# Planning an instruction order with longer elementwise durations and fewer reserved PSUM banks

## The chip, the cores and the metric

The kernel runs on one core of one Trainium2 chip. The metric is the device time of one launch in microseconds (us), as the median of three timed runs. A profile is one more execution, recorded by the hardware; its engines are called PE (TensorE, matrix products), PEld (its weight loads), DVE (VectorE), ACT (ScalarE), POOL (GpSimd) and SP (the queue that issues the DMAs).

## The reference

Two networks run one after the other on 512 tokens of width 1024, two layers each. In the first, a layer mixes latent attention (8 heads) with a gated depthwise convolution of 31 taps, and is followed by a gated feed-forward of width 2816. The second has a state-space mixer in its first layer, a gated recurrence (HGRN2) in its second, and after each a squared-ReLU feed-forward of width 4096 and a gate by an embedding. Cut to what matters:

```python
for l in range(DEPTH):
    p = _rmsnorm(x, g_mix[l]) @ w_in[l]
    c_q, c_kv = _rmsnorm(p[..., :o1], g_q[l]), _rmsnorm(p[..., o1:o2], g_kv[l])
    y_attn = _mla_attention(q_nope, q_rope, k_nope, k_rope, v)      # from c_q @ w_uq, c_kv @ w_ukv
    u = _dwconv(a * jax.nn.sigmoid(gt), w_dw_conv[l], b_dw_conv[l])  # 31 taps
    u = jax.nn.silu(_layernorm(u, g_conv_ln[l], b_conv_ln[l]))
    x = x + jnp.concatenate([y_attn, u], axis=-1) @ w_o[l]
    z = _dwconv(_rmsnorm(x, g_ffn[l]) @ w_up[l], w_dw_ffn[l], b_dw_ffn[l])
    x = x + (jax.nn.silu(zg) * zv) @ w_down[l]
x = _rmsnorm(x, g_final)
for i in range(DEPTH):
    mix = ssd_mixer(x, ...) if i % 2 == 0 else hgrn2_mixer(x, ...)
    h = layer_norm(ALPHA * x + mix, ...)
    h = layer_norm(ALPHA * h + relu(h @ w1)**2 @ w2, ...)
    x = h + jax.nn.sigmoid(h @ ple_w_gate[i]) * (p[i] @ ple_w_proj[i])
```

## The kernel before

All activations are held transposed: 128 channels on the partitions, 512 tokens along a row, so the stream X is eight tiles of 128x512. A weight block comes by one DMA into one of three buffers of class `r` (the function `weights`, line 687) and is then split into a high part, a cast to the rounded format fp32r (`copy`, line 684: on ScalarE or on VectorE), and a low part, the difference (`either.tensor_sub`: on GpSimd or on VectorE). A dense product is, per 128 rows of weight, three matmuls (high by high, high by low, low by high) that add up in one PSUM bank: 24 for a full sum over 1024 channels. When its sum is complete, VectorE or ScalarE reads the bank.

Nothing is issued while the network is written down. The class `Recorder` only notes operations with the tiles that they read and write, and `schedule` (line 462) then plans all 19,079 of them: it holds a time at which each engine is free, takes again and again the ready operation that could start earliest (ties and near ties by a priority made of recording order and length of what follows), adds its planned cost, and hands out the buffers. `issue` (line 587) emits the instructions in that order, so every elementwise instruction, matmul and DMA in the profile stands on line 597. On the chip each engine works off its own queue in the planned order and waits where the order makes it wait; the plan's times are not used any further.

Three things in the planner matter here. First, `cost` (line 342) gives the planned duration of an operation on ScalarE, VectorE or GpSimd; `cost_tensor` gives that of matmuls and is another function. Second, an operation recorded with `either`, `other` or `any` may run on one of two engines; the second of them is taken only if the operation ends there no later than it would on the first, by what is already queued on both. In this way casts go between ScalarE and VectorE, and two-source additions, subtractions and products between GpSimd and VectorE. Third, `KEEP` (line 616) says how many of a class's free buffers a younger operation must leave for tiles that were recorded earlier and have none yet; there are eight PSUM banks, and the number kept is four.

In the attention part, a head pair runs through Q and K products, score blocks of 128x512 (three matmuls into a bank), a minimum over a row on VectorE, an exponential on ScalarE, transposes on TensorE, copies out of PSUM, and the products with V. Beside it `conv_tile` (line 976) works off the convolution: 17 taps accumulate in a PSUM bank on VectorE (SCALAR_TENSOR_TENSOR psum<-u,V,psum), 14 are multiplied on ScalarE (ACTIVATE s<-u,V) and added by GpSimd or VectorE. The output projection follows, first for the attention's half, then for the convolution's half after a normalisation. In the recurrence (`hgrn`, line 1316), every head forms decay products over six levels before its small matmuls. Normalisations over 1024 channels and the last projection before them are done in two halves of 256 tokens.

Of the kernel before, what the change touches and what calls it, by code (L numbers as in the profile page):

```python
# [232 lines left out]
class Tl:  # L233


    def __init__(self, cls, shape, dt):
        self.cls, self.shape, self.dt = cls, tuple(shape), dt
        self.acc, self.left, self.slot, self.real, self.pe = [], 0, None, None, None
        self.touch = {}
# [80 lines left out]
class Recorder:  # L320
# [9 lines left out]
    def __init__(self):  # L330
        self.ops, self.bias, self.label, self.switch = [], 0, "", 150
        self.greed, self.order_w, self.second, self.eager, self.drag = 0.015, 1.0, 0, 0, 0.5

    def tile(self, cls, shape, dt=F32):
        return Tl(cls, shape, dt).ap()
# [4 lines left out]
        return _Eng(self, eng)  # L340

    def cost(self, eng, meth, args, kw):
        out = kw.get("out", args[0] if args else None)
        n = out.n if isinstance(out, Ap) else 1
        every = [a for a in list(args) + list(kw.values()) if isinstance(a, Ap)]
        ps = any(a.tl.cls == "psum" for a in every)
        ptr = sum(isinstance(a, Ap) and a.n == 1 for a in args[1:]) + sum(isinstance(kw.get(k), Ap) for k in ("scale", "bias"))
        if eng == "scalar":
            return (51 if ps else 93) + 0.833 * n + 93 * (ptr + ("accum_out" in kw))
        if eng == "vector":  # L350
            if meth == "reciprocal":
                return 70 + 6.3 * n
            if meth in ("tensor_scalar", "tensor_copy") and not ps:
                return 69 + 0.52 * n + 60 * ptr
            if meth == "tensor_reduce":
                n = kw["in_"].n
            return 69 + 1.041 * n + 60 * ptr
        if eng == "gpsimd":
            if kw.get("op") == ALU.pow:
                return 298 + 165 * n  # L360
            if meth == "memset":
                return 36 + n
            if meth == "tensor_copy":
                return 120 + 3.4 * n
            return 147 + 2.105 * n
        return 60
# [32 lines left out]
    def any(self, *forms):  # L399

        eng, meth, args, kw = forms[0]
        self.add(eng, meth, args, kw)
        self.ops[-1].alts = [(e, self.cost(e, m, a, k), [(m, a, k)]) for e, m, a, k in forms]
        self.ops[-1].shared = {e: self.shares(e, m, a, k) for e, m, a, k in forms}
# [208 lines left out]


SLOTS = {"psum": 8, "r": 3, "s": 86, "u": 4, "t": 12, "n": 24, "V": 1, "C": 1}
KEEP = {"psum": 4, "s": 18, "u": 2, "t": 6, "n": 16}
SIDE_TAPS = 14
EARLY = 3
FILL = {"mlp0": [(0, 0)], "mlp1": [(1, 0)]}
# [994 lines left out]
def build(tc, xT, pos, wts, vecs, consts, pT, outT, dbg=None, stop=None):  # L1614
    R = Recorder()
    record(R, xT, pos, wts, vecs, consts, pT, outT, dbg, stop)
    R.schedule(SLOTS, KEEP)
    with tc.manual_schedule(), tc.tile_pool(name="sbuf", bufs=1) as sb, \
# [37 lines left out]
```

## Time and profile before

| | us |
|---|---|
| median of three timed runs (2746.51 to 2747.91) | 2747.29 |
| profiled execution, its own time | 2746.72 |
| its span, first to last instruction | 2744.9 |
| TensorE busy in the span | 2680.1 |
| VectorE busy | 1878.6 |
| ScalarE busy | 1176.4 |
| GpSimd busy | 775.2 |

The mean granted clock of TensorE is 0.995 of full speed; a view by stretch ends each row with that clock, the DMA share and GB/s. A group of instructions is read as: line, engine, operation, what is written and read by buffer class (`s` tiles of up to 2 KB a partition, `r` raw weights, `u` padded rows, `n` and `t` small ones, `V` per-channel vectors, `C` constants, `psum`), size and count. Matmuls overlap in the records, so a busy TensorE is not always one at its full rate. The profile's slices show a nearly full TensorE everywhere; the places where it is not full are two stretches near the start and near 700 us, and parts of 1200 to 1450 and 1950 to 2350 us.

### The profile page before, as it was taken

Reading aid. Unit: us, or ns where it says so; the run is one execution under the profiler, and the core shown is the slowest. Engines: PE = TensorE matmul, PEld = TensorE weight load, DVE = VectorE, ACT = ScalarE, POOL = GpSimd, SP = SyncE. Lnnn points to the kernel's source line nnn. Section 1 sums busy time; section 2 is a strip of 40 time slices with the busy share of each in tenths; the row PEclk is TensorE's granted clock in tenths of the full one; section 3 lists DMA queues with packets and bytes.
Section 4 is the critical chain, followed back from the end, with each engine's and each line's share of the span. In section 5 each row is a group of like instructions: output and inputs, shape, how many; then the busy total and the mean of one; then the engine's idle time right before and its main releaser. Section 6 shows DMA issues by size and latency. Waiting matters only on the chain.

```text
span 2744.9 us, 38876 instructions
## 1 busy us (share of the span) xinstructions
PE 2680.1 (98%) x15054; PEld 2213.4 (81%) x15054; DVE 1878.6 (68%) x3319; ACT 1176.4 (43%) x2151; POOL 775.2 (28%) x645
## 2 busy tenths in 40 slices
PE   9899999999899999999989999999999999999998
PEld 7668888888678888888768898888888889888888
DVE  8997676666977766675885675445677887554546
ACT  4874323345764332343653432222356664322223
POOL 1771010134840111242331421222412123112232
PEclk9999999999999999999999999999999999999999
DMA  5031233231131223331112413223131113232320
GB/s 171 18 108 69 76 103 107 99 111 30 56 108 54 93 92 108 99 103 47 40 62 73 163 55 103 91 101 109 62 108 48 60 66 114 88 108 83 115 93 32
DMA packets 69448, 234.98 MB, mean 86 GB/s; under 512 B 7824, under 2 KB 11152, under 8 KB 69264
## 3 DMA queue, kind: packets, MB, share of 16 engines
q1 hardware_dynamic: 69264, 232.51, 25.3%
q8 instruction: 118, 1.93, 0.3%
q14 instruction: 66, 0.54, 0.1%
HBM read 230.38 MB, written 2.10 MB: 85 GB/s over the span
## 4 chain that ended last, share of the span: by engine, by line
PE 80%; DVE 15%; issue 3%; ACT 2%; POOL 0%; DMA 0%; POOLq 0%; DVEq 0%; ACTq 0%; SPq 0%
PE psum L597 80%; DVE s L597 10%; DVE psum L597 3%; ACT s L597 1%; DVE n L597 1%; ACT L597 0%; DMA r<-wts 0%; POOL n L597 0%; POOL s L597 0%; DVE u L597 0%; DVE t L597 0%; POOL u L597 0%; ACT t L597 0%; POOLq L597 0%; DVEq L597 0%
## 5 line engine op out<-in xcount | busy, mean ns | idle before, releaser
L597 PE MATMUL psum<-s,s 128*128 128x512 f32 (+3 forms) x12944 | 2604.2, 365 | 35.8 <-DVE s L597 16.0
L597 PEld LDWEIGHTS psum<-s,s 128*128 128x128 f32 (+1 forms) x12944 | 2117.8, 185 | 472.8 <-issue 27.3
L597 POOL TENSOR_TENSOR s<-r,s 128x512 fp32r<-128x512 f32 (+1 forms) x342 | 469.4, 1389 | 1062.2 <-ACT s L597 798.7
L597 ACT CAST s<-r 128x512 fp32r<-128x512 f32 (+1 forms) x721 | 407.9, 611 | 402.3 <-DMA r<-wts 390.4
L597 DVE TENSOR_TENSOR s<-s,s 128x256 f32<-128x256 f32 (+5 forms) x625 | 405.8, 672 | 76.7 <-ACT s L597 66.1
L597 DVE TENSOR_TENSOR s<-s,psum 128x512 f32<-128x512 f32 (+2 forms) x400 | 224.0, 591 | 297.6 <-PE psum L597 297.2
L597 POOL TENSOR_TENSOR s<-s,s 128x512 f32<-128x512 f32 (+4 forms) x215 | 257.1, 1206 | 514.2 <-DVE s L597 348.3
L597 DVE TENSOR_TENSOR s<-r,s 128x512 fp32r<-128x512 f32 (+1 forms) x527 | 378.2, 746 | 5.9 <-ACT s L597 3.4
L597 ACT ACTIVATE s<-s 128x512 f32<-128x512 f32 (+1 forms) x338 | 186.5, 579 | 211.8 <-DVE s L597 210.6
L597 ACT ACTIVATE s<-u,V 128x512 f32<-128x512 f32 x200 | 142.5, 763 | 264.8 <-DVE u L597 264.6
L597 ACT ACTIVATE s<-psum 128x512 f32<-128x512 f32 (+2 forms) x174 | 91.7, 528 | 373.6 <-PE psum L597 370.3
L597 DVE SCALAR_TENSOR_TENSOR s<-u,V,s 128x512 f32<-128x512 f32 x176 | 143.1, 814 | 50.0 <-ACT s L597 46.8
L597 DVE SCALAR_TENSOR_TENSOR s<-psum,s 128x512 f32<-128x512 f32 (+1 forms) x88 | 55.3, 639 | 113.4 <-ACT s L597 109.4
L597 DVE TENSOR_TENSOR u<-psum,s 128x512 f32<-128x512 f32 x88 | 60.6, 689 | 83.0 <-PE psum L597 82.8
L597 POOL TENSOR_TENSOR n<-n,n 128x4 f32<-128x4 f32 (+1 forms) x32 | 35.0, 1095 | 282.1 <-DVE n L597 281.6
L597 ACT COPY s<-psum 128x512 f32<-128x512 f32 (+4 forms) x137 | 69.6, 531 | 86.2 <-PE psum L597 85.2
L597 ACT CAST s<-s 128x512 fp32r<-128x512 f32 (+2 forms) x125 | 72.7, 592 | 75.4 <-DVE s L597 74.7
L597 DVE CAST s<-r 128x512 fp32r<-128x512 f32 (+1 forms) x148 | 62.7, 434 | 54.5 <-DMA r<-wts 54.3
L597 ACT ACT_TABLE_LOAD x68 | 87.2, 1283 | 21.2 <-DVE s L597 19.3
L597 PE MATMUL psum<-C,s 128*128 128x128 f32 (+1 forms) x532 | 80.3, 271 | 12.7 <-ACT s L597 6.0
L597 DVE SCALAR_TENSOR_TENSOR psum<-u,V,psum 128x512 f32<-128x512 f32 x128 | 91.3, 743 | 0.3
L597 PEld LDWEIGHTS psum<-C,s 128*128 128x128 f32 x532 | 63.6, 146 | 30.7 <-ACT s L597 12.8
(87 smaller groups left out, 875.3 us busy)
## 6 DMA issues: line engine op xcount, KB each, us to landing
r<-wts SPq DMA_DIRECT2D x415, 512.0 KB, 3.6
r<-wts SPq DMA_DIRECT2D x12, 256.0 KB, 2.8
r<-wts SPq DMA_DIRECT2D x8, 384.0 KB, 3.1
s<-xT SPq DMA_DIRECT2D x8, 256.0 KB, 6.1
s<-pT SPq DMA_DIRECT2D x8, 256.0 KB, 4.0
outT<-s SPq DMA_DIRECT2D x16, 128.0 KB, 1.8
r<-wts SPq DMA_DIRECT2D x9, 128.0 KB, 2.0
V<-vecs SPq DMA_DIRECT2D x1, 480.5 KB, 6.6
```

Of the source, the lines that this page charges most:

```text
L597: getattr(eng, meth)(*[res(a) for a in args], **{k: res(v) for k, v in kw.items()})
```

## The change

A new attribute `margin` of 1.1 multiplies the planned duration of everything on ScalarE, VectorE and GpSimd. The old formulas move unchanged into `duration`; the cost of matmuls and of DMAs stays as it is. `KEEP` for PSUM goes from four to two. Nothing else is edited, so the operations recorded are the same, and their order and, where there is a choice, their engine are planned anew.

```diff
--- before.py
+++ after.py
@@ -330,6 +330,7 @@
     def __init__(self):
         self.ops, self.bias, self.label, self.switch = [], 0, "", 150
         self.greed, self.order_w, self.second, self.eager, self.drag = 0.015, 1.0, 0, 0, 0.5
+        self.margin = 1.1
 
     def tile(self, cls, shape, dt=F32):
         return Tl(cls, shape, dt).ap()
@@ -340,6 +341,11 @@
         return _Eng(self, eng)
 
     def cost(self, eng, meth, args, kw):
+
+        return self.duration(eng, meth, args, kw) * (1.0 if eng == "sync" else self.margin)
+
+    @staticmethod
+    def duration(eng, meth, args, kw):
         out = kw.get("out", args[0] if args else None)
         n = out.n if isinstance(out, Ap) else 1
         every = [a for a in list(args) + list(kw.values()) if isinstance(a, Ap)]
@@ -613,7 +619,7 @@
 
 
 SLOTS = {"psum": 8, "r": 3, "s": 86, "u": 4, "t": 12, "n": 24, "V": 1, "C": 1}
-KEEP = {"psum": 4, "s": 18, "u": 2, "t": 6, "n": 16}
+KEEP = {"psum": 2, "s": 18, "u": 2, "t": 6, "n": 16}
 SIDE_TAPS = 14
 EARLY = 3
 FILL = {"mlp0": [(0, 0)], "mlp1": [(1, 0)]}
```

What the new plan does is seen in the order in which instructions stand on an engine. A name is a buffer class and a number that tells tiles apart; the numbers differ between the two kernels.

VectorE in the first layer, up to the addition that completes the sum of squares of the key-value latent (`s_885<-s_885,s_922` in the last row). `psum_620` and `psum_691` are the convolution's accumulators of channel tiles 0 and 1; `s_908<-psum_749,V_65,s_890` is the low part of a latent. Before:

```order
L597 SCALAR_TENSOR_TENSOR psum_620<-u_71,V_65,psum_620 128x512
L597 SCALAR_TENSOR_TENSOR psum_691<-u_67,V_65,psum_691 128x512
L597 SCALAR_TENSOR_TENSOR psum_620<-u_71,V_65,psum_620 128x512
L597 TENSOR_TENSOR s_585<-s_585,s_737 128x512
L597 SCALAR_TENSOR_TENSOR psum_620<-u_71,V_65,psum_620 128x512
L597 TENSOR_SCALAR n_905<-psum_887 128x4
L597 SCALAR_TENSOR_TENSOR s_908<-psum_749,V_65,s_890 128x512
L597 TENSOR_TENSOR n_905<-n_905,n_525 128x4
L597 SCALAR_TENSOR_TENSOR psum_620<-u_71,V_65,psum_620 128x512
L597 SCALAR_TENSOR_TENSOR psum_691<-u_67,V_65,psum_691 128x512
L597 TENSOR_SCALAR n_905<-n_905 128x4
L597 TENSOR_TENSOR s_885<-s_885,s_922 128x512
```

The same place with the change; the addition is `s_863<-s_863,s_891` in the last row, `psum_603` the accumulator of channel tile 0:

```order
L603 TENSOR_SCALAR s_391<-s_391,V_65 128x512
L603 TENSOR_SCALAR s_449<-s_449,V_65 128x512
L603 SCALAR_TENSOR_TENSOR s_857<-s_758,V_65,s_391 128x512
L603 SCALAR_TENSOR_TENSOR s_865<-s_789,V_65,s_449 128x512
L603 TENSOR_TENSOR s_873<-r_555,s_802 128x512
L603 TENSOR_SCALAR n_878<-psum_860 128x4
L603 SCALAR_TENSOR_TENSOR s_880<-psum_731,V_65,s_869 128x512
L603 SCALAR_TENSOR_TENSOR psum_603<-u_71,V_65,psum_603 128x512
L603 TENSOR_TENSOR n_878<-n_878,n_681 128x4
L603 TENSOR_TENSOR s_863<-s_863,s_891 128x512
```

Fewer convolution taps stand ahead of that addition; it was instruction 153 of VectorE's queue and is 139. The rotary tables (`s_391`, `s_449`) are finished later than before.

TensorE at the end of the attention of layer 1. `psum_7080` takes the last products of probabilities and V, `psum_7139` the convolution's mean, `psum_7169` and `psum_7181` are the first sums of the output projection. Before:

```order
L597 MATMUL psum_7130<-C_156,s_7111 128x128 x4
L597 MATMUL psum_7139<-s_6663,t_78 128x512
L597 MATMUL psum_7080<-s_7120,s_6115 64x256
L597 MATMUL psum_7080<-s_7132,s_6115 64x256
L597 MATMUL psum_7080<-s_7120,s_6210 64x256
L597 MATMUL psum_7080<-s_7132,s_6210 64x256
L597 MATMUL psum_7080<-s_7123,s_6226 64x256
L597 MATMUL psum_7080<-s_7136,s_6226 64x256
L597 MATMUL psum_7080<-s_7123,s_6233 64x256
L597 MATMUL psum_7080<-s_7136,s_6233 64x256
L597 MATMUL psum_7169<-s_6497,s_6398 128x512
L597 MATMUL psum_7169<-s_6527,s_6398 128x512
```

The same place with the change: the products go to `psum_7052`, the convolution's mean to `psum_7102`, the output projection's sums are `psum_6920` and `psum_7112`:

```order
L603 MATMUL psum_7093<-C_152,s_7076 128x128 x4
L603 MATMUL psum_7102<-s_7065,t_78 128x512
L603 MATMUL psum_7112<-s_6490,s_6475 128x512
L603 MATMUL psum_6920<-s_6737,s_6475 128x512
L603 MATMUL psum_7112<-s_6498,s_6475 128x512
L603 MATMUL psum_7052<-s_7087,s_6164 64x256
L603 MATMUL psum_7052<-s_7106,s_6164 64x256
L603 MATMUL psum_7052<-s_7087,s_6170 64x256
L603 MATMUL psum_7052<-s_7106,s_6170 64x256
L603 MATMUL psum_7052<-s_7095,s_6185 64x256
L603 MATMUL psum_7052<-s_7110,s_6185 64x256
```

Matmuls of the output projection now stand ahead of the last products of attention; the very first of `psum_6920` stands 77 instructions further up.

GpSimd in the recurrence, at its last heads. Rows with `r` are low parts of weights, `n` a power of four columns, a shape of three numbers is an operation on half of a tile's columns. Before:

```order
L597 TENSOR_TENSOR s_20300<-s_20300,s_20180 128x64x4
L597 TENSOR_TENSOR n_20391<-n_20386,n_74 128x4
L597 TENSOR_TENSOR s_20425<-r_20176,s_20419 128x512
L597 TENSOR_TENSOR s_20653<-s_20653,s_20514 128x512
L597 COPY s_20704<-s_20657 128x256
L597 TENSOR_TENSOR s_20704<-s_20708,s_20786 128x256
L597 TENSOR_TENSOR n_20932<-n_20928,n_74 128x4
L597 TENSOR_TENSOR s_20939<-r_20359,s_20757 128x512
L597 TENSOR_TENSOR s_20962<-r_20538,s_20804 128x512
L597 TENSOR_TENSOR n_21122<-n_21110,n_74 128x4
```

The same heads with the change:

```order
L603 TENSOR_TENSOR s_20285<-s_20285,s_20195 128x16x16
L603 TENSOR_TENSOR n_20396<-n_20387,n_74 128x4
L603 TENSOR_TENSOR s_20355<-s_20355,s_20195 128x8x32
L603 TENSOR_TENSOR s_20433<-s_20417,n_20293 128x4x64
L603 TENSOR_TENSOR s_20671<-r_20281,s_20655 128x512
L603 COPY s_20693<-s_20543 128x256
L603 TENSOR_TENSOR s_20735<-s_20735,s_20543 128x32x8
L603 TENSOR_TENSOR n_20928<-n_20925,n_74 128x4
L603 TENSOR_TENSOR s_20824<-s_20824,s_20543 128x8x32
L603 TENSOR_TENSOR s_20954<-s_20931,n_20766 128x4x64
L603 TENSOR_TENSOR s_20970<-s_20941,n_20766 128x4x64
L603 TENSOR_TENSOR n_21118<-n_21103,n_74 128x4
```

More of the heads' half-tile products stand on GpSimd, which were on VectorE.

## Rows read from the trace of the kernel before

**Rows 1.** The page: TensorE's busy time; the chain that ended last, by engine.

```profile
PE 2680.1 (98%) x15054; PEld 2213.4 (81%) x15054; DVE 1878.6 (68%) x3319; ACT 1176.4 (43%) x2151; POOL 775.2 (28%) x645
...
PE 80%; DVE 15%; issue 3%; ACT 2%; POOL 0%; DMA 0%; POOLq 0%; DVEq 0%; ACTq 0%; SPq 0%
```

**Rows 2.** Stretches: from, to, length, busy us (instructions) of PE, PEld, DVE, ACT, POOL.

```profile
45.00:200.00 155.00, 141.20 (x719) 104.79 (x719) 152.28 (x238) 119.64 (x233) 104.93 (x85) 0.98 0.16 54
200.00:640.00 440.00, 439.95 (x1917) 357.72 (x1916) 294.87 (x439) 155.35 (x256) 74.76 (x62) 1.00 0.28 95
640.00:750.00 110.00, 101.50 (x503) 78.41 (x501) 102.79 (x160) 82.88 (x155) 82.01 (x70) 1.00 0.10 31
750.00:800.00 50.00, 47.81 (x278) 36.08 (x279) 39.12 (x62) 35.13 (x74) 27.42 (x20) 1.00 0.30 98
...
1200.00:1440.00 240.00, 228.87 (x1317) 183.58 (x1316) 184.75 (x389) 125.55 (x203) 84.97 (x70) 0.99 0.15 49
2030.00:2280.00 250.00, 241.62 (x2986) 207.70 (x2985) 191.87 (x463) 169.68 (x326) 55.96 (x42) 0.99 0.21 69
```

**Rows 3.** What TensorE waited for, whole span: us in total, times, longest us.

```profile
PE psum L597 <- DVE s L597: 24.9, 30, 3.3
PE psum L597 <- ACT s L597: 15.6, 23, 1.7
...
PE psum L597 <- POOL s L597: 4.3, 7, 1.1
```

**Rows 4.** The same, 45 to 200 us.

```profile
PE psum L597 <- ACT s L597: 5.7, 7, 1.1
PE psum L597 <- DVE s L597: 4.9, 3, 3.3
```

**Rows 5.** The same, 640 to 800 us.

```profile
PE psum L597 <- ACT s L597: 4.0, 6, 1.7
...
PE psum L597 <- POOL s L597: 1.2, 2, 0.7
```

**Rows 6.** The same, 1200 to 1440 us.

```profile
PE psum L597 <- DVE s L597: 6.9, 10, 1.1
```

**Rows 7.** The same, 2030 to 2280 us.

```profile
PE psum L597 <- issue: 6.5, 3, 2.5
```

**Rows 8.** Timeline near 96 us: start, us, engine, instruction [idle before <- releaser].

```profile
95.80 0.67 DVE L597 TENSOR_TENSOR s<-s,s 128x512 f32<-128x512 f32 x1
...
96.52 1.05 PE L597 MATMUL psum<-C,s 128*128 128x1 f32 x8 [3.35 <-DVE s L597]
```

**Rows 9.** Timeline near 697 us.

```profile
696.99 1.09 PE L597 MATMUL psum<-C,n 128*128 128x128 f32 x8 [3.32 <-DVE n L597]
```

**Rows 10.** Groups of VectorE by shape, whole span: busy us, mean ns | idle before.

```profile
L597 DVE TENSOR_TENSOR s<-r,s 128x512 fp32r<-128x512 f32 x518 | 374.8, 752 | 5.9 <-ACT s L597 3.4 <-PE psum L597 0.5
...
L597 DVE TENSOR_TENSOR s<-s,s 128x256 f32<-128x256 f32 x196 | 87.0, 471 | 28.8 <-ACT s L597 24.6 <-POOL s L597 2.8
L597 DVE CAST s<-s 128x512 fp32r<-128x512 f32 x89 | 64.1, 720 | 4.1 <-DVE s L597 0.5
L597 DVE CAST s<-r 128x512 fp32r<-128x512 f32 x146 | 62.1, 436 | 53.5 <-DMA r<-wts 53.3
```

**Rows 11.** Groups of GpSimd and ScalarE by shape, whole span.

```profile
L597 POOL TENSOR_TENSOR s<-s,s 128x512 f32<-128x512 f32 x111 | 155.2, 1409 | 156.8 <-DVE s L597 89.2 <-ACT s L597 52.8 <-PE psum L597 10.7
L597 POOL TENSOR_TENSOR s<-s,s 128x256 f32<-128x256 f32 x50 | 41.1, 832 | 123.9 <-DVE s L597 67.6 <-ACT s L597 56.3
...
L597 ACT ACT_TABLE_LOAD x68 | 87.2, 1283 | 21.2 <-DVE s L597 19.3 <-PEq L1648 0.7
```

**Rows 12.** Timeline near 108 us: a VectorE subtraction beside GpSimd.

```profile
106.62 2.58 POOL L597 TENSOR_TENSOR s<-s,s 128x512 fp32r<-128x512 f32 x2 [1.57 <-DVE s L597]
106.73 1.41 DVE L597 SCALAR_TENSOR_TENSOR psum<-u,V,psum 128x512 f32<-128x512 f32 x2
...
108.05 1.72 DVE L597 TENSOR_TENSOR s<-r,s 128x512 fp32r<-128x512 f32 x1
```

## The prediction

> **What bounds the kernel now.** I read the page first: TensorE is busy 98% of the span, and the chain that ended last lies on it for 80% and on VectorE for most of the rest [rows 1]. So elementwise durations can only matter where TensorE is not fed, and the second view, busy time by stretch, says where that is [rows 2]. In 200 to 640 us, mostly the first feed-forward, TensorE has no gap worth naming and VectorE is busy 67%; the other three feed-forward parts look alike. No order of elementwise work can win time there. The first attention with its convolution (45 to 200 us) is different: VectorE is busy 152.3 of 155 us, TensorE 141.2. The second one begins alike (640 to 750: 102.8 of 110), with a loose end (750 to 800: 39.1 of 50). The state-space block (1200 to 1440) has VectorE at 77% and TensorE idle for 11.1 us; the gated recurrence (2030 to 2280) has 8.4 us of idle TensorE.
>
> The third view is what TensorE waited for. Of its waits VectorE's tiles ended 24.9 us, ScalarE's 15.6 and GpSimd's 4.3 [rows 3]. In the first attention 4.9 us end on VectorE and 5.7 on ScalarE [rows 4]; but VectorE itself is idle only 2.7 us there, so ScalarE's lateness is mostly VectorE's, one step back, and in this stretch time is what VectorE has queued. A row shows it: the four-column sums of the key-value latent start at 96.52 us after 3.35 us of idle TensorE, released by an addition that VectorE began at 95.80 [rows 8], behind convolution taps that nobody waits for yet. At 696.99 us the same happens in the second layer, 3.32 us [rows 9].
>
> **The change part by part.** No operation is added or removed, only placed. Counted along the queues, VectorE has 3200 instructions instead of 3319, ScalarE 2044 instead of 1987 (table loads apart), GpSimd 703 instead of 641, TensorE and the DMA queue as many as before. So planning with longer elementwise durations makes VectorE's backlog look longer and sends casts to ScalarE and two-source operations to GpSimd.
>
> *First attention.* Ahead of the last subtraction of attention 0, VectorE has 297 instructions instead of 310. 37 are gone: 11 casts and copies, 25 two-source operations, one small copy. 24 came: 6 casts (one of half width) and 18 two-source (one of half width). A two-source operation takes 0.75 us, a cast 0.44 (from a weight buffer) to 0.72 (from a tile), mean 0.58 [rows 10]. So 5.5 x 0.58 = 3.2, and 7.5 x 0.75 = 5.6: 8.8 us less. TensorE's work up to that point is the same to two matmuls. Since VectorE has 2.7 idle us of 155, nothing hides this; I take 7, as the chain score, minimum, exponential, transposes keeps some of it (ScalarE ends seven of TensorE's waits there [rows 4]). Bounds 0 and 8.8.
>
> *Second attention.* Between the last residual of the first feed-forward and the last subtraction of attention 1 it is 226 instead of 236: 34 gone (15 casts, 19 two-source), 24 came (7 and 17, one half): 8 x 0.58 + 2.5 x 0.75 = 6.5 us. Only the first two thirds are bound by VectorE [rows 2], so I take 4.5. Bounds 0 and 6.5.
>
> *State-space block.* 358 instead of 372 between the second feed-forward and the last result of the block: ten two-source and four casts fewer, some 7.5 us of VectorE. It is not full there; TensorE waits 6.9 us for it [rows 6]. I take 2, bounds 0 and 6.9.
>
> *Gated recurrence.* VectorE loses 32 instructions, GpSimd gains 12, most of them half-width products of the decay levels. Of the 8.4 us that TensorE idles there 6.5 are "issue", which has no elementwise releaser [rows 7]. Value 0; what this side can lose is a rival below.
>
> *Two banks kept instead of four.* TensorE may open younger sums while older ones are still to come. The places are the ends of attention, where output-projection matmuls now stand ahead of the last score block's products. A 512-column matmul costs 0.23 us (1917 instructions in 440 us [rows 2]), and the ones moved are a handful, all paid anyway: their worth is that they fill gaps already counted above. Zero by itself, bounds -2 and +2.
>
> *Table loads.* 72 instead of 68, 1.28 us each [rows 11]: 5.1 us of ScalarE, two of them in the state-space block and two in the recurrence, where ScalarE has 114 of 240 and 80 of 250 us free [rows 2]. Nothing; 5.1 if that cover were gone.
>
> *Normalisations and start.* VectorE's queue has the same operations, a few swapped. Outside the first attention and the state-space block TensorE waits 24.9 - 4.9 - 6.9 = 13.1 us for VectorE's tiles [rows 3, 4, 6], most of it here. Value 0, and I allow 4 either way, a third of that.
>
> The sum: 7 + 4.5 + 2 = 13.5 us. The profiled execution took 2746.72 us, 1.8 of it outside its span of 2744.9, and lies 0.6 below the median of the three timed runs. 2746.7 - 13.5 = 2733.2, with the median's offset 2733.8; I say 2733.5.
>
> **The rivals.** *A: VectorE's share comes off whole.* 8.8 + 6.5 + 6.9 = 22.2 us, 2725. For it: VectorE's 98% in the first attention. Against: the second is loose after 750 us.
>
> *B: no change.* VectorE gets done sooner and then waits for scores, as the chain through TensorE, VectorE's minimum, ScalarE's exponential and the transposes sets the pace. Then all terms are zero: 2747. For it: ScalarE ends 5.7 us of TensorE's waits in attention and 4.0 in the second [rows 4, 5]. Against: with VectorE at 98% there is no sign of a pace that is not its own.
>
> *C: GpSimd becomes the late one, slower.* A two-source operation takes 1.41 us there against 0.75 [rows 10, 11], so each moved one comes 0.66 later to its reader, and while it runs VectorE can be held: a two-source operation that started beside one took 1.72 instead of 0.75 [rows 12]. Moved to GpSimd are 21 in the first attention and 18 in the second (18 and 16 others come back). If the moved ones are on the chain: 21 x 0.66 - 8.8 = +5.1, 18 x 0.66 - 6.5 = +5.4, and 13 half-width products of the recurrence at 0.83 instead of 0.47 [rows 10, 11]: +4.7. Together +15.2: 2762. It decides once GpSimd has no free time before a reader needs it: it is busy 104.9 of 155 and 82.0 of 110 us [rows 2], so a third is free. Against it also: TensorE waited for GpSimd's tiles 1.2 us in the second attention [rows 5] and 4.3 in the whole span, and GpSimd's queue up to its last operation of attention 0 is two instructions shorter than before.
>
> The Trainium skill (SBUF, "Who interferes with whom") says that a VectorE instruction with two SBUF inputs and a GpSimd instruction that reads SBUF exclude each other, the first one holding the pair of ports for its whole length; the row of 1.72 us agrees. By that rule, if the pair of ports were what fills the first attention, a net three operations moved to GpSimd would lengthen it by 3 x 0.66 = 2.0 us instead of winning 7, and the sum would be 2742; it is a mild form of C and has its chance there. Against it stands a row: two taps, which read one tile and a PSUM bank, took 1.41 us beside GpSimd [rows 12], 0.7 each, so much of VectorE's work in attention does not meet GpSimd's.
>
> **How the numbers follow.** Forecast 0.55, A 0.12, B 0.15, C 0.18. The forecast's own range is 2726 to 2741, gains of 6 to 21 of the 22.2 that the bounds allow. The range of 8 in 10 reaches over B to the weaker half of C, in which only one attention stretch and the recurrence pay: 2720 to 2754. This kernel's runs agree to some 0.05%, and 0.2% (5.5 us) is what I take as told from no change: faster is under 2741.8. A and nearly all of the forecast give 0.66; B with the forecast's weak end 0.16; C 0.18.
>
> **What will show it.** If right: TensorE's wait of 3.35 us at 96.5 and of 3.32 at 697 are gone or halved; the transposes that stood at 696.99 us stand some 8 us earlier, 7 from the first attention and the rest from their own; VectorE is still over 93% busy in the first attention; TensorE has no gaps in the feed-forward parts, as before. Wrong: VectorE under 90% there with no shorter stretch (B); TensorE's waits for GpSimd's tiles grown from 4.3 us to over 12, or the recurrence longer than 255 us (C). Those transposes at 697 us or later would break the main term.

## The result, and the profile after

The changed kernel takes 2721.65 us (median of four runs, 2720.93 to 2726.2), the kernel before, run beside it, 2746.9 (2743.84 to 2747.91). The ratio is 0.9913, 95% interval 0.9896 to 0.9931: faster by 0.9%, or 25 us. The forecast was 2733.5 in a range of 2720 to 2754, so the time lies in the lower end of the range: below the forecast's own range (2726 to 2741), and some 3 us below rival A (2725).

The profiled execution of the changed kernel is the slowest of its four, 2726.2 us with a span of 2724.4. The traces therefore show 20.5 of the 25 us. The page after, where [rows 1] showed the page before:

```profile
PE 2672.7 (98%) x15054; PEld 2214.5 (81%) x15054; DVE 1835.5 (67%) x3200; ACT 1216.5 (45%) x2212; POOL 851.9 (31%) x707
...
PE 91%; DVE 6%; issue 1%; ACT 1%; DMA 1%; POOL 0%; SPq 0%; POOLq 0%; DVEq 0%; ACTq 0%
```

VectorE's part of the chain that ended last fell from 15% to 6%. By stretch, answering to [rows 2] (from, to, length, busy us of PE, PEld, DVE, ACT, POOL with their counts, granted clock, DMA share, GB/s); the bounds are moved to about where the same work lies now:

```profile
45.00:188.00 143.00, 135.29 (x712) 102.19 (x712) 137.87 (x223) 115.70 (x224) 101.37 (x82) 1.00 0.12 41
188.00:628.00 440.00, 439.86 (x1920) 358.24 (x1919) 299.78 (x438) 164.43 (x273) 89.02 (x70) 1.00 0.30 101
628.00:728.00 100.00, 97.63 (x484) 76.10 (x483) 88.67 (x143) 78.04 (x147) 68.44 (x60) 1.00 0.07 23
728.00:778.00 50.00, 49.95 (x297) 37.70 (x296) 44.01 (x69) 39.49 (x85) 35.39 (x30) 1.00 0.27 95
1178.00:1415.00 237.00, 227.56 (x1319) 182.93 (x1319) 179.13 (x378) 130.03 (x208) 91.68 (x78) 0.99 0.15 50
2005.00:2256.00 251.00, 244.04 (x2984) 210.80 (x2983) 184.74 (x436) 176.75 (x336) 65.45 (x55) 0.98 0.19 64
```

VectorE is still 96% busy in the first attention (137.87 of 143), and the stretch is shorter. The end of the second attention has lost its slack: TensorE is busy 49.95 of 50 us, where it was 47.81. The feed-forward has no gap, as before.

What TensorE waited for in the whole span, in 45 to 240 us, in 600 to 840 and in 1180 to 1440 (us in total, times, longest), answering to [rows 3 to 6]:

```profile
PE psum L603 <- DVE s L603: 24.2, 28, 4.2
PE psum L603 <- ACT s L603: 11.2, 17, 1.4
PE psum L603 <- issue: 6.9, 4, 2.3
...
PE psum L603 <- POOL s L603: 1.2, 3, 0.4
...
PE psum L603 <- ACT s L603: 5.0, 9, 1.2
PE psum L603 <- DVE s L603: 2.4, 3, 1.0
...
PE psum L603 <- DVE s L603: 1.5, 3, 0.6
PE psum L603 <- ACT s L603: 0.4, 2, 0.2
...
PE psum L603 <- DVE s L603: 5.8, 9, 1.7
```

The two waits that the prediction hung on are gone. The timeline of the changed kernel at the four-column sums and at the transposes of the second layer [rows 8, 9]:

```profile
86.31 0.68 DVE L603 TENSOR_TENSOR s<-s,s 128x512 f32<-128x512 f32 x1
...
87.31 0.95 PE L603 MATMUL psum<-C,s 128*128 128x1 f32 x8
...
680.53 0.60 PE L603 MATMUL psum<-C,n 128*128 128x128 f32 x4
```

Neither matmul has an idle time in brackets behind it now. Of the eight transposes that stood at 696.99 us four now stand 16.5 us earlier, the other four 14.2; the prediction said 8.

A third wait is gone that the prediction did not name. Within the stretch of [rows 4] TensorE also waited 2.5 us for a small tile of GpSimd's, before the transposes of the first normalisation; the row, and the timeline of the kernel before:

```profile
PE psum L597 <- POOL n L597: 2.5, 1, 2.5
...
44.64 0.95 PE L597 MATMUL psum<-C,s 128*128 128x1 f32 x8
...
48.26 0.15 DVE L597 TENSOR_SCALAR n<-psum 128x4 f32<-128x4 f32 x1
...
50.55 1.11 PE L597 MATMUL psum<-C,n 128*128 128x128 f32 x4 [2.53 <-POOL n L597]
```

and of the changed kernel:

```profile
44.16 0.95 PE L603 MATMUL psum<-C,s 128*128 128x1 f32 x8
...
45.14 0.16 DVE L603 TENSOR_SCALAR n<-psum 128x4 f32<-128x4 f32 x1
...
48.07 0.60 PE L603 MATMUL psum<-C,n 128*128 128x128 f32 x4
```

GpSimd was late mainly because VectorE was: before, VectorE read TensorE's sum 2.7 us after it was complete, behind products for the rotary tables; now it reads it at once.

A view that the prediction left out shows more. The granted clock of the kernel before, in windows of 5 us (the third number from the right; 1.00 is 2.4 GHz, 0.50 would be 1.2 GHz throughout):

```profile
50.00:55.00 5.00, 4.45 (x15) 3.74 (x16) 4.47 (x7) 2.50 (x3) 4.10 (x4) 0.66 0.31 103
...
95.00:100.00 5.00, 3.48 (x16) 2.90 (x17) 4.86 (x11) 5.00 (x10) 4.04 (x6) 0.81 0.00 0
97.00:102.00 5.00, 5.00 (x19) 4.04 (x19) 4.86 (x10) 5.00 (x10) 5.00 (x7) 0.66 0.00 2
100.00:105.00 5.00, 5.00 (x22) 4.12 (x21) 4.36 (x11) 2.56 (x5) 3.89 (x3) 0.85 0.00 2
```

and of the changed kernel at the same work:

```profile
85.00:90.00 5.00, 5.00 (x28) 4.20 (x27) 5.00 (x14) 4.52 (x8) 1.34 (x2) 1.00 0.25 79
90.00:95.00 5.00, 5.00 (x26) 3.96 (x25) 4.96 (x9) 4.62 (x9) 2.33 (x2) 1.00 0.00 0
```

After the wait of 3.35 us TensorE had work without a break, but in 97 to 102 us the granted clock was 0.66, so 1.7 us (5 x 0.34) of the full clock were missing. The matmuls show the same amount:

```profile
97.44 6.87 PE L597 MATMUL psum<-s,s 128*128 128x512 f32 x22
```

At 0.23 us each, as in the feed-forward, these 22 would have taken 5.1 us and not 6.87. The window from 50 to 55 us stands behind the wait of 2.53 us and lacks as much. So a wait can cost twice, its own length and slow matmuls behind it, and here the change took away both.

To see where the time went, I cut all traces at the same operations. Each entry is the length of the stretch in us, and in brackets TensorE's idle time and the time missing to the full clock (length times one minus the granted clock, summed over windows of 10 us; where TensorE also idles in such a window, the two overlap). One profiled run each; "margin" is the factor 1.1 with four banks kept, "banks" two banks kept with factor 1.0, "early" the factor 1.1 in the first network's attention parts alone with two banks kept; they are experiments of the next section.

| stretch, up to | before | after | margin | banks | early |
|---|---|---|---|---|---|
| end of output projection 0 | 245.5 (17.4, 5.1) | 234.5 (12.0, 1.7) | 241.2 (14.3, 6.9) | 248.9 (20.0, 8.5) | 236.1 (12.5, 1.7) |
| feed-forward 0 | 367.3 | 366.3 | 366.7 | 367.5 | 366.4 |
| output projection 1 | 224.5 (10.7, 0) | 213.8 (2.4, 0) | 217.1 (4.7, 1.7) | 225.2 (8.6, 5.1) | 213.4 (2.0, 0) |
| feed-forward 1 | 365.9 | 366.5 | 365.8 | 366.1 | 365.9 |
| state-space block | 227.5 (10.5, 1.7) | 224.7 (8.4, 1.7) | 231.0 (11.7, 5.1) | 224.5 (8.2, 1.7) | 224.5 (8.3, 1.7) |
| its output projection | 173.5 | 172.0 | 172.2 | 172.7 | 173.0 |
| third feed-forward | 364.7 | 365.6 | 367.6 | 366.0 | 365.0 |
| first embedding gate | 62.8 (3.0, 3.4) | 67.3 (5.2, 6.8) | 63.1 (3.4, 3.4) | 66.5 (4.9, 5.2) | 66.6 (4.9, 5.1) |
| recurrence with its output | 287.5 (9.2, 1.7) | 284.8 (7.6, 5.1) | 280.5 (7.3, 0) | 289.8 (10.5, 1.7) | 289.8 (9.3, 3.4) |
| last feed-forward | 364.3 | 364.5 | 366.0 | 365.1 | 364.4 |
| last gate | 58.6 | 61.2 | 60.4 | 60.1 | 61.2 |

So the change wins 11.0 and 10.7 us in the two attention parts, some 1.5 to 3 in each of three later stretches, and gives back 4.5 at the first embedding gate and 2.6 at the last. TensorE's idle time and its low clock account for most of the difference in the attention parts: over the 14 kernels of this study the second of them ranges from 212.4 to 232.3 us, and length less the two bracketed numbers only from 209.6 to 214.9. In the first part they make 8.8 of the 11.0 us (5.4 of idle time and 3.4 of clock).

### The profile page after: what moved, and what is told of

The parts are those of the page before. It is cut to its first block, busy times and chain, and to the rows that moved or that the text cites. A ratio compares the mean times of both kernels' runs of the same rounds, so it can differ in the third digit from the quotient of the medians.

```text
span 2724.4 us, 38893 instructions
## 1 busy us (share of the span) xinstructions
PE 2672.7 (98%) x15054; PEld 2214.5 (81%) x15054; DVE 1835.5 (67%) x3200; ACT 1216.5 (45%) x2212; POOL 851.9 (31%) x707
## 4 chain that ended last, share of the span: by engine, by line
PE 91%; DVE 6%; issue 1%; ACT 1%; DMA 1%; POOL 0%; SPq 0%; POOLq 0%; DVEq 0%; ACTq 0%
PE psum L603 91%; DVE s L603 4%; ACT s L603 1%; DVE psum L603 1%; DVE n L603 1%; DMA r<-wts 0%; POOL s L603 0%; DMA s<-xT 0%; POOL n L603 0%; SPq L603 0%; POOLq L603 0%; DVEq L603 0%; ACTq L603 0%
## 5 line engine op out<-in xcount | busy, mean ns | idle before, releaser
L603 PE MATMUL psum<-s,s 128*128 128x512 f32 (+5 forms) x12944 | 2600.4, 365 | 26.3 <-DVE s L603 13.7
L603 PEld LDWEIGHTS psum<-s,s 128*128 128x128 f32 (+2 forms) x12944 | 2119.7, 186 | 454.6 <-issue 28.2
L603 POOL TENSOR_TENSOR s<-r,s 128x512 fp32r<-128x512 f32 (+1 forms) x375 | 516.6, 1394 | 1046.6 <-ACT s L603 810.1
L603 ACT CAST s<-r 128x512 fp32r<-128x512 f32 (+1 forms) x739 | 420.0, 612 | 366.8 <-DMA r<-wts 343.3
L603 DVE TENSOR_TENSOR s<-s,s 128x512 f32<-128x512 f32 (+5 forms) x603 | 389.2, 668 | 94.0 <-ACT s L603 85.4
L603 POOL TENSOR_TENSOR s<-s,s 128x512 f32<-128x512 f32 (+5 forms) x237 | 278.1, 1184 | 478.2 <-ACT s L603 299.5
L603 DVE TENSOR_TENSOR s<-r,s 128x512 fp32r<-128x512 f32 x494 | 360.9, 758 | 9.0 <-ACT s L603 6.3
L603 ACT CAST s<-s 128x512 fp32r<-128x512 f32 (+2 forms) x152 | 90.0, 597 | 110.7 <-DVE s L603 109.4
L603 ACT ACT_TABLE_LOAD x72 | 92.4, 1283 | 13.8 <-DVE s L603 6.4
L603 DVE CAST s<-r 128x512 fp32r<-128x512 f32 (+1 forms) x130 | 56.2, 446 | 44.7 <-DMA r<-wts 44.5
```

Source lines behind the costliest of these rows:

```text
L603: getattr(eng, meth)(*[res(a) for a in args], **{k: res(v) for k, v in kw.items()})
```

## The experiments

**First set: the parts, and places against order.** The theory was that VectorE's shorter queue (the places) makes the gain; the rivals, that the banks do, or the order as such.

The factor alone:

```diff
-KEEP = {"psum": 2, "s": 18, "u": 2, "t": 6, "n": 16}
+KEEP = {"psum": 4, "s": 18, "u": 2, "t": 6, "n": 16}
```

> The factor 1.1 alone, four PSUM banks kept. Relief theory (VectorE has less in its queue during attention and is held less by GpSimd; this comes from the factor): 2726 to 2732 us. Bank theory (TensorE runs ahead because fewer banks are kept, and that is the gain): 2742 to 2748 us. If both are needed: 2735 to 2740.

Measured: 2737.55 us, ratio 0.9953 [0.9939, 0.9968], about half of the gain.

The banks alone:

```diff
-        self.margin = 1.1
+        self.margin = 1.0
```

> Two PSUM banks kept alone, durations as planned before. Relief theory: 2741 to 2747 us, VectorE's instruction count near 3319. Bank theory: 2722 to 2730 us with TensorE's gaps between 640 and 800 us filled by output-projection matmuls.

Measured: 2756.66 us, ratio 1.0026 [1.0017, 1.0036], slower. The two parts do not add up: -0.47% and +0.26% make -0.87% together.

The engine choices of the one plan with the order of the other: the operations are planned once, every choice is nailed to the engine it got (`place_as`), and the whole is planned again with the other factor and number of banks.

```diff
+    def place_as(self, other):
+        for o, q in zip(self.ops, other.ops):
+            if len(o.alts) > 1:
+                o.alts = [x for x in o.alts if x[0] == q.eng]
+                o.eng, o.cost, o.calls = o.alts[0]
...
+    Q, R = Recorder(1.1), Recorder(1.0)
...
+    Q.schedule(SLOTS, dict(KEEP, psum=2))
+    R.place_as(Q)
+    R.schedule(SLOTS, dict(KEEP, psum=4))
```

> Each operation on the engine that the changed plan chose, but the order planned with the durations and the four kept banks of before. Relief theory with placement as its cause: 2726 to 2733 us. Order theory (the sequence is what gains, the engines hardly matter): 2742 to 2749 us.

Measured: 2758.67 us, ratio 1.003 [1.002, 1.004]. And the other way round, with the 1.0 and the 1.1, the 4 and the 2 exchanged:

> The counterpart: engines as chosen before, order planned with the factor 1.1 and two kept banks. Relief theory with placement as its cause: 2738 to 2746 us. Order theory: 2720 to 2728 us.

Measured: 2759.41 us, ratio 1.0029 [1.0017, 1.0041]. The theory in its simple form fell with these two: the new choices lose with an order planned at the old factor and banks, and so do the old choices with an order planned at the new ones. They do not tell places from order, though. Neither has the order of the other kernel, but a new one, and with the choices nailed the planner makes a worse plan by its own reckoning: its planned end (what `schedule` returns) is 2701 us where the kernel before has 2672 at the same factor and banks, and 2726 where the changed kernel has 2690. In the first of them VectorE has 304 instructions ahead of the last subtraction of attention 0, fewer than the 310 of before, yet TensorE waited there for one VectorE tile for 12.1 us (45 to 250 us):

```profile
PE psum L610 <- DVE n L610: 12.7, 2, 12.1
```

and the clock fell during it and stayed down behind it:

```profile
90.00:100.00 10.00, 4.49 (x20) 3.30 (x18) 10.00 (x17) 9.74 (x18) 10.00 (x10) 0.91 0.05 14
100.00:110.00 10.00, 3.43 (x12) 3.17 (x13) 9.14 (x16) 4.99 (x9) 8.36 (x8) 0.50 0.00 1
```

What stands ahead of the operation that TensorE waits for matters, and the number of instructions in the queue is only a part of that. The banks alone show the same: in the stretch from 45 to 240 us TensorE waited longer for VectorE than before [rows 4], and the matmuls at 117.53 us follow the longest of these waits:

```profile
PE psum L603 <- DVE s L603: 12.6, 6, 6.5
```

on the timeline:

```profile
117.53 5.03 PE L603 MATMUL psum<-s,s 128*128 128x512 f32 x11 [6.47 <-DVE s L603]
```

and the granted clock of the 10 us around it and of the next 10:

```profile
110.00:120.00 10.00, 3.52 (x11) 2.58 (x10) 9.70 (x8) 4.32 (x7) 7.10 (x7) 0.65 0.00 1
120.00:130.00 10.00, 9.78 (x44) 7.53 (x43) 8.66 (x15) 6.57 (x17) 1.23 (x4) 0.84 0.01 2
```

**Second set: a systematic gain, or a lucky order?** After the first set it could be that any edit draws another order, and 1.1 with two banks drew well. Neighbouring factors, the factor in one part of the program, and a nearly neutral edit tell that.

```diff
-        self.margin = 1.1
+        self.margin = 1.09
```

> Factor 1.09 instead of 1.1, two banks kept. Theory S (systematic): a longer planned duration thins VectorE's queue, and the queue sets the time of the attentions; up to the last subtraction of attention 0 VectorE has 300 instructions here (297 with 1.1, 310 before), in the second attention 229 (226, 236). So nearly all of the gain stays: ratio to before 0.990 to 0.994. Theory D (draw): any edit of the planner draws another order, and orders scatter by some tenths of a per cent whatever the counts; 1.1 with two banks is a good draw. Then 1.09 is worth what its draw gives, on average what the margin alone gave: 0.994 to 1.000.

Measured: 2729.0 us, ratio 0.9929 [0.9913, 0.9945]. With 1.11 in place of 1.09:

> Factor 1.11, two banks kept: VectorE has 299 instructions up to the last subtraction of attention 0, 233 in the second attention (310 and 236 before, 297 and 226 with 1.1). Theory S: ratio 0.990 to 0.994. Theory D: 0.994 to 1.000, and not the same as 1.09.

Measured: 2726.62 us, ratio 0.9918 [0.9903, 0.9933]. Both as theory S had it, and the draw's range (0.994 to 1.000) is missed by both medians. The second attention part takes 216.8 and 213.1 us (213.8 with 1.1), the state-space block 224.4 and 226.2 (224.7); the first attention part scatters more, 236.7 and 239.1 (234.5).

The factor in the first network's mixers alone:

```diff
-        return self.duration(eng, meth, args, kw) * (1.0 if eng == "sync" else self.margin)
+        return self.duration(eng, meth, args, kw) * (self.margin if self.label.rstrip("01") in ("in", "att", "conv", "wo") else 1.0)
```

> Factor 1.1 only for operations recorded in the input projections, attentions, convolutions and output projections of the first network, 1.0 elsewhere, two banks kept. VectorE has 297 instructions up to the last subtraction of attention 0, as with the whole change, 228 in the second attention, and 363 in the state-space block (358 with the change, 372 before). Theory S (the two attentions make the gain): the last residual of the first output projection some 10 us earlier than before, the last residual of the second one some 20, and the end 17 to 26 us earlier, ratio 0.990 to 0.994, since the later stages gave and took about the same. Theory D: the marks of the first network elsewhere than with the whole change, and a ratio between 0.995 and 1.003.

Measured: 2731.39 us, ratio 0.9934 [0.9917, 0.9951]. The last residual of the first output projection is 9.4 us earlier than before and that of the second 21.4, as theory S had it; the end is 16.0 earlier in the profiled runs, just short of its 17 to 26, and 17.8 by the medians side by side. Most of the gain is made in these two parts; without the factor the recurrence stays at 289.8 us. In the state-space block it has 363 VectorE instructions against 358 with the whole change, and the block takes the same time (224.5 and 224.7 us).

The nearly neutral edit, a factor of 1.01 with four banks:

```diff
-        self.margin = 1.1
+        self.margin = 1.01
...
-KEEP = {"psum": 2, "s": 18, "u": 2, "t": 6, "n": 16}
+KEEP = {"psum": 4, "s": 18, "u": 2, "t": 6, "n": 16}
```

> Factor 1.01, four banks kept: nearly the plan of before (VectorE 3336 instructions instead of 3319; 311 and 240 in the two attentions instead of 310 and 236). A measure of how far orders scatter when nothing of weight is changed. Theory S: VectorE has a few instructions more, so the same or a little slower: 0.999 to 1.003. Theory D: off by 0.2 to 0.5% either way.

Measured: 2752.41 us, ratio 1.0011 [1.0002, 1.0021], as S had it in sum. But its first attention part is 6.5 us shorter than before with one instruction more on VectorE, and later stretches lose it again. So single stretches do scatter by some us with an edit of no weight. The first attention part is no shorter with 1.11 (239.1 us) than with this edit (239.0), so its gain of 11 us with 1.1 may in part be that; the second one, 223.6 us here, is not shorter without the factor.

**Third set: which durations, and how many banks.** VectorE alone planned slower:

```diff
-        return self.duration(eng, meth, args, kw) * (1.0 if eng == "sync" else self.margin)
+        return self.duration(eng, meth, args, kw) * (self.margin if eng == "vector" else 1.0)
```

> Factor 1.1 for VectorE alone, ScalarE and GpSimd planned at 1.0; two banks kept. VectorE has 295 instructions up to the last subtraction of attention 0 and 222 in the second attention (297 and 226 with the whole change, 310 and 236 before). Theory S, in the form that VectorE's planned backlog is what matters: as good as the whole change, ratio 0.988 to 0.994. Rival E (the longer planned durations help because tiles of all three engines come later than planned, so their readers on TensorE must be placed later): ScalarE and GpSimd, planned too short against a longer VectorE, get more than they can do in time, and most of the gain goes, 0.996 to 1.003.

Measured: 2736.22 us, ratio 0.9951 [0.9936, 0.9966], between the two theories. The second attention part is the shortest of all, 212.4 us, with VectorE's shortest queue (222). The first one wins nothing, 245.3 us, though its queue is the shortest as well (295): TensorE waited 6.0 us for VectorE and 6.1 for ScalarE (45 to 240 us):

```profile
PE psum L603 <- ACT s L603: 6.1, 6, 2.5
PE psum L603 <- DVE s L603: 6.0, 7, 1.7
```

and the granted clock was down in these windows among others:

```profile
160.00:170.00 10.00, 7.41 (x36) 4.69 (x35) 10.00 (x17) 5.01 (x11) 10.00 (x12) 0.83 0.16 54
180.00:190.00 10.00, 7.46 (x38) 6.09 (x38) 9.70 (x13) 6.00 (x15) 6.83 (x9) 0.89 0.15 52
190.00:200.00 10.00, 10.00 (x66) 6.74 (x66) 8.17 (x15) 9.07 (x20) 4.12 (x4) 0.94 0.46 158
```

So in the second part the factor on VectorE's durations is enough. The number of instructions in the queue does not say why: with 229 of them that part took 216.8 us at 1.09, and 232.3 in the first of the two nailed kernels. In the first part it may also matter that ScalarE's and GpSimd's work is planned as late as it really comes, or that part is one draw: the runs don't tell these apart.

One bank kept, and three (only the number in `KEEP` differs from the change):

```diff
-KEEP = {"psum": 2, "s": 18, "u": 2, "t": 6, "n": 16}
+KEEP = {"psum": 1, "s": 18, "u": 2, "t": 6, "n": 16}
```

> Factor 1.1, one bank kept. If fewer kept banks let younger sums fill gaps of the attentions, one bank keeps the gain of two: 0.989 to 0.994. If two is a good draw among orders that scatter by 0.2%, anything from 0.990 to 0.997. By the instruction counts alone (304 and 233 in the two attentions, near those of four banks, 302 and 231) it would be near four banks, 0.994 to 0.996.

Measured: 2729.7 us, ratio 0.9922 [0.9903, 0.9941].

> Factor 1.1, three banks kept. If the banks work by filling gaps, between four banks (0.9953) and two (0.9913), so 0.991 to 0.996; by the counts (303 and 228 in the two attentions) 0.993 to 0.996; by a draw of orders anything from 0.990 to 0.998.

Measured: 2738.7 us, ratio 0.9961 [0.9946, 0.9975]. With the factor at 1.1, the ratios for four, three, two and one bank are 0.9953, 0.9961, 0.9913 and 0.9922: one step, between three and two, and the forecast by instruction counts (0.994 to 0.996 for one bank) fell. The state-space block shows the step by itself: 231.0 and 229.6 us with four and three banks, 224.7 and 224.5 with two and one, and 224.5 with two banks and no factor. The first embedding gate shows it the other way: 63.1 us with four, 65.9 with three, 67.3 and 66.7 with two and one.

A larger factor:

```diff
-        self.margin = 1.1
+        self.margin = 1.2
```

> Factor 1.2, two banks kept. VectorE 300 and 227 in the two attentions, 366 in the state-space block (358 with 1.1). Theory S: the counts stop falling at 1.1, so the gain of the attentions stays and no more comes: 0.990 to 0.994. Rival E (readers placed later because tiles come later than planned): 1.2 leaves too much slack, work of TensorE is put off, and 1.2 is worse than 1.1 by 0.2% or more, 0.993 to 0.999.

Measured: 2751.16 us, ratio 1.0002 [0.9992, 1.0011]. The whole gain is gone, beyond what either theory gave it, though VectorE's queues are nearly as short as with 1.1 (300 and 227 after 297 and 226). In the first part, 244.8 us, TensorE idles 18.1 us and lacks 10.4 to the full clock; at the first embedding gate, 75.7 us, it waits twice for a long time, here on the timeline:

```profile
1965.66 1.22 PE L603 MATMUL psum<-s,t 128*128 128x256 f32 x2 [5.63 <-DVE s L603]
...
1976.31 1.22 PE L603 MATMUL psum<-s,s 128*128 128x512 f32 x2 [9.43 <-DVE s L603]
```

and the clock is at its lower level between the two:

```profile
1970.00:1980.00 10.00, 3.69 (x14) 3.30 (x15) 7.79 (x23) 1.41 (x4) 0.71 (x1) 0.50 0.00 0
```

Why the planner puts so much ahead there with 1.2 was not traced.

**The 14 kernels side by side.** The second attention part separates kernels with the factor from those without, one profiled run each: the nine kernels planned freely with a factor of 1.09 or more on VectorE there take 212.4 to 220.1 us, the other five 223.6 to 232.3. In the first part the two groups overlap (234.5 to 245.3 and 239.0 to 248.9).

One reason for a factor near 1.1 lies in the record and was not tested. Where a VectorE instruction of the kernel before follows the last one without a gap, the time from start to start is on average 1.09 times what the planner had put down for it (1.11 in the first attention), and on GpSimd 1.11 times (1.14); this is an estimate from the starts in the trace and the costs in `duration`. So 1.1 comes near to the durations of the chip, 1.01 and 1.2 do less so, and neither of these two gained. A plan with each shape's own measured duration was not run, nor was ScalarE compared.

## Why the prediction was right, and where it was not

The places of the gain were right and most of the sizes were not. The two attention terms were too small by 10.2 us together, and losses of 7.1 us at the two embedding gates, put at nothing, took most of that back: that the time stayed in the range is partly luck. Rival A comes nearest in time, but by another sum: its 6.9 us for the state-space block measured 2.8, its 8.8 and 6.5 for the attentions 11.0 and 10.7.

*Where the time would come from: right.* Both waits that it named are gone, VectorE is still over 93% busy in the first attention, the feed-forward parts don't move, and the experiment with the factor in the first network's mixers alone shows that the two attention parts carry most of the gain. Rival B fell, and C too: TensorE's waits for GpSimd's tiles went from 4.3 us [rows 3] to 1.2 (for its small ones from 3.5 to 1.3), not above 12, and the recurrence is shorter (287.5 to 284.8), not longer.

*First attention, 7 us (bounds 0 and 8.8): 11.0.* The step that failed is the pricing of VectorE's queue alone. The operation that the counts of 310 and 297 run up to, VectorE's last product of that attention (the subtraction behind it is GpSimd's in both kernels), stands 9.7 us earlier. At the median duration of each shape the queue shrank by some 7 us (196 to 189) where the prediction had 8.8; single operations also overran their median less, by some 13 us in sum after 17. TensorE's idle time tells it more directly: the waits of 3.35 and of 2.53 us together are a little more than the 5.4 us that it idles less. The second of them is missing from the prediction's rows. And 3.4 of the 11.0 is time missing to the full clock, 5.1 before and 1.7 after, which the prediction did not look at although the row of that stretch shows 0.98 [rows 2]. The experiments take from the mechanism as stated, too: with fewer VectorE instructions still (295), the part took 245.3 us. A queue length is not a time; what stands ahead of the awaited tile matters.

*Second attention, 4.5 us (bounds 0 and 6.5): 10.7.* The step "only the first two thirds are bound by VectorE" counted the loose end as worth nothing. TensorE idled 10.7 us in this part and idles 2.4 now, and in its last 50 us there is no gap left. In the single profiled runs the factor alone makes 7.4 of it; the rest comes with the two banks.

*State-space block, 2 us: 2.8, but for another reason.* The prediction put it to 14 VectorE instructions less. With the factor and four banks the block has 359 instead of 372 and takes 3.5 us longer than before; with two banks and no factor it has 363 and takes 3.0 less. Over the freely planned kernels the block takes 227.5 to 231.0 us with four or three banks kept, 224.2 to 227.0 with two or one. The term has the right size and a wrong cause: it is the banks.

*Recurrence, 0: 2.7 us shorter.* The factor alone makes 7.0 of it and the banks cost 2.3; all eight freely planned kernels with the factor in that part take 280.5 to 286.4 us, the five without it (or with 1.01) 287.5 to 289.8. TensorE's waits there hardly change (issue 6.5 and 6.9), so where these us come from stays open.

*Two banks, zero by itself (bounds -2 and +2): wrong.* By itself +0.26%, some 7 us slower; with the factor, 0.9953 to 0.9913 in ratios, each against the kernel before beside it, some 11 us faster. The prediction's bound treated it as one effect that adds to the others. That it does not is shown by these runs; why the factor turns its sign is not.

*Normalisations and start, 0 (4 either way).* At the first normalisation VectorE reads the sum 3.1 us earlier (45.14 after 48.26), which is part of the 11.0 above; at the two embedding gates the change loses 4.5 and 2.6 us. The first of these losses is the banks': 66.5 us with the banks alone and 66.6 in the kernel whose plan has no factor there, 63.1 with the factor alone. The timeline of the changed kernel shows a wait of 4.21 us there:

```profile
1948.46 1.22 PE L603 MATMUL psum<-s,t 128*128 128x256 f32 x2 [4.21 <-DVE s L603]
...
1952.77 7.62 PE L603 MATMUL psum<-s,s 128*128 128x256 f32 x31 [0.96 <-DVE s L603]
...
1960.37 2.15 PE L603 MATMUL psum<-s,s 128*128 128x256 f32 x16
```

and this window the low clock behind it:

```profile
1950.00:1955.00 5.00, 4.04 (x18) 3.58 (x17) 5.00 (x17) 3.53 (x10) 2.52 (x3) 0.50 0.00 0
```

At a granted clock of 0.50 the 256-column matmul takes 7.62 / 31 = 0.25 us, and 2.15 / 16 = 0.13 once it is back at 1.00. Before, the wait at this place was 2.30 us.

*Table loads, 0: not contradicted.* There are 72 of 1283 ns, as forecast, and ScalarE's waits ended less of TensorE's idle time than before (11.2 after 15.6 us).

The rule of the Trainium skill (SBUF, "Who interferes with whom") that spoke against the change is the pair of ports that VectorE and GpSimd share. As the prediction worked it out, the first attention would have become 2.0 us longer. It became shorter, although GpSimd is now busy 71% of that stretch (101.37 of 143 us) after 68%; so waits at that pair of ports did not decide the stretch's length.

From the table a version suggests itself that keeps two banks up to the state-space block and four from there: the gate at 63.1 instead of 67.3 and the recurrence at 280.5 instead of 284.8 would be 8.5 us, of which the third and the last feed-forward and the last gate together take back 2.7 (1137.6 us in all five with the factor alone, 1143.4 with the change), an estimate from single profiled runs. It was not run.

## What to carry to other kernels

When an order is planned from costs, test a factor on those costs at neighbouring values and in one stage alone before believing it: here 1.09, 1.1 and 1.11 agree within 0.2%, 1.2 gives everything back, and two edits that cost and win by themselves can win more together. Look up the granted clock in short windows behind every wait of the matmul engine, since a wait may cost well above its own length. A queue that is shorter by some instructions is a reason to expect a gain, not its size: ask what stands ahead of the operation that the busy engine waits for, on whichever engine the wait ends.

## What the runs showed of the hardware

The granted clock of TensorE was down behind waits of 2.3 to 3.4 us (0.66 in 97 to 102 us of the kernel before, with TensorE busy in all of it), and not behind every one: the 3.32 us at 697 us left it at 1.00, in a window from 697 to 702 us:

```profile
697.00:702.00 5.00, 5.00 (x26) 4.04 (x26) 4.96 (x10) 3.87 (x8) 4.51 (x4) 1.00 0.00 0
```

In its profiled run the changed kernel lacks more to the full clock than the one before (18.7 against 13.6 us by the sums of the table's method) and is faster all the same, since it idles less (48.4 against 62.1 us). How much is missing differs from run to run of the same kernel: the profiled run has a mean granted clock of 0.993 and a span of 2724.4 us, the other three 0.994 to 0.996 and 2719.2 to 2720.2.
